# Where the weight tiles stand relative to the activation tiles, modulo 256 bytes

## The chip, the cores and the metric

One core of a Trainium2 chip runs the whole program. The metric is the device time of one execution in microseconds. Three executions of the kernel before took 1433.52, 1434.24 and 1435.65 us, median 1434.24 us.

## What is computed

Two transformer blocks of two layers each follow each other on 256 positions of width 1,024, in float32. Cut to the matrix products, one layer of the first block is:

```python
proj = rms_norm(x) @ w_in                      # 1024 x 5120
y = gate_a * (dilated_attention(...) @ w_proj_a) + gate_b * (stick_breaking_attention(...) @ w_proj_b)
x = x + y @ w_out                              # 1024 x 1024
up = rms_norm(x) @ w_up                        # 1024 x 5632
x = x + (silu(conv(up[:, :2816])) * up[:, 2816:]) @ w_down   # 2816 x 1024
...
x = x + norm(mixer(norm(x)))                   # second block, two kinds of mixer
x = x + norm(memory_cross_attention(norm(x), mem))
x = x + norm(square(relu(norm(x) @ mlp_w1)) @ mlp_w2)        # 1024 x 4096, 4096 x 1024
```

Every weight is used once, so the weights (some 230 MB) are read from HBM once per execution.

## The kernel before, in words

**Layout.** Activations lie transposed, with the 1,024 features on partitions in eight chunks of 128 and the 256 positions along the free dimension. All big products run on TensorE in the type float32r, in three terms: each operand is held as a rounded part (hi) and the rest (lo), and `mm3` (L240 to L243) issues hi x hi, lo x hi and hi x lo into the same bank, each through `mm` (L235, whose matmul is L236).

**Weights.** `plan()` lists the weights in 434 blocks in the order of use, each 512 KB or less. `prep` (L188 to L201) loads one block by DMA into a `raw` tile (three buffers), cuts it in two halves along the contraction, and for each half makes a tile `w`: ScalarE writes the hi part (L199), VectorE the lo part (L200). There are eight slots for `w` (`WB`, L35), taken in turn. A `w` tile holds up to 4,096 bytes a partition; in one pair of blocks (260 columns) it holds 4,160, and so all eight slots have that size. `take` (L203) hands a block's tiles to the product and `ahead` (L211) keeps `prep` five blocks (`LEAD`) in front.

**The products.** In `proj_t` (L288) the weights are the stationary operand (128 columns, loaded anew by each matmul) and the activations the moving one (256 columns). One `w` tile serves 12 matmuls in a row, one turn of the eight slots 96. So run the 22 pairs of `w_up` in two layers (1,056 matmuls a layer), the 16 of `w1` in two layers (768 a layer), the gates of `w_in`, and most products of the mixers. `proj_wide` (L324), used by `proj_tail` for `w_out`, `w_down` and `w2`, alternates a matmul of 512 columns (hi and lo of the activations at once) with one of 256, a pair for each 128 rows of the contraction. In `proj_n` (L334) the activations are stationary and the weights move (512 columns).

**Addresses.** Activations as operands of these products are `xh` tiles of two pools of slots: `xs` (four slots, the normalised input, L615 and `operand`) and `hs` (16 slots, everything else: `ya`, `yb`, `ox`, `lat`, the hidden layers). A slot's address within a partition is fixed when the program is built. In the built program before, the first `w` slot stands at byte 39,552 and the others each 4,160 bytes on, so modulo 256 the eight stand at 128, 192, 0, 64, 128, 192, 0, 64. All `xs` slots stand at 128 and all `hs` slots at 64. The tiles' inner offsets (hi, lo, chunk, column block) are all multiples of 256. So what this text calls the **distance** of a `w` tile from the activations it meets (its address minus theirs, modulo 256) is 0, 64, 128 or 192, the same for all the matmuls of that tile, and each occurs in two of eight slots. The profile shows no addresses; which distance a stretch has is read from the order of the built program.

Small tiles of softmax and norms are in 16 slots `sm` (L642 to L675 and others), each as large as the largest of them, `ra` and `rb` of the rotary embedding (`rope_unit`, L671; 512 bytes).

Of the kernel before, what the change touches and what calls it, by code (L numbers as in the profile page):

```python
# [10 lines left out]
F32 = mybir.dt.float32  # L11
F32R = mybir.dt.float32r
# [7 lines left out]
P = 128  # L20
# [12 lines left out]
TWO_PI = (6.28125, 0.0019350051879882812, 3.0199159819567e-07)  # L33
LEAD = 5
WB = 8  # L35
TCARGS = dict(schedule_with_timeline_sim=True)
SET_EXP = "natural_log_exp_and_others"

# [77 lines left out]
def starts(blocks):  # L116

    out = [0]
    for _, _, nk, _, C in blocks:
# [1 line left out]
    return out  # L121


BUFS = {"x": 5, "xs": 4, "hs": 16, "ft": 7, "sq": 2, "p": 6, "bias": 3, "row": 4, "sm": 16, "mk": 2, "mv": 2,
        "mm": 2, "sc": 2, "pT": 2, "pv": 1, "ms": 1}


# [1 line left out]
def net(ctx, tc, A, out):  # L129
# [3 lines left out]
    wp = ctx.enter_context(tc.tile_pool(name="wts", bufs=1))  # L133
    ap = ctx.enter_context(tc.tile_pool(name="acts", bufs=1))
    pp = ctx.enter_context(tc.tile_pool(name="psum", bufs=1, space=PSUM))
    dp = ctx.enter_context(tc.tile_pool(name="dram", bufs=1, space=DRAM))

    def f(x):
        return x.bitcast(F32)

    def sb(tag, name, shape=(2, T), dt=F32):
        return ap.tile([P] + list(shape), dt, tag=tag, name=name, bufs=BUFS[tag])

    halves = {}

    def single(group, name):

        if group in halves:
            return halves.pop(group)
        t = ap.tile([P, 2, 2, T], F32, tag="hs", name=name, bufs=BUFS["hs"])  # L150
        halves[group] = t[:, 1]
        return t[:, 0]

    def split_pair(tag, name):

        return ap.tile([P, 2, 2, T], F32R, tag=tag, name=name, bufs=BUFS[tag])

    def bank(tag, name, shape=(2, T), part=P):
        return pp.tile([part] + list(shape), F32, tag=tag, name=name, bufs=BUFS[tag])

# [27 lines left out]
    def prep(i, pieces=1):  # L188
        name, k0, nk, c0, C = W[i]
        raw = wp.tile([P, nk, C], F32, tag="raw", name=f"raw{i}", bufs=3)  # L190
        src = A["wt"][start[i]:start[i] + P * nk * C].rearrange("(p k c) -> p k c", p=P, k=nk)
        for a in range(0, nk, max(1, nk // pieces)):
            nc.sync.dma_start(raw[:, a:a + max(1, nk // pieces)], src[:, a:a + max(1, nk // pieces)])
        h = max(1, nk // 2)
        ready[i] = []
        for a, b in ((0, h), (h, nk)):
            if a < b:
                w = wp.tile([P, 2, b - a, C], F32R, tag="w", name=f"w{i}", bufs=WB)
                act.activation(w[:, 0], raw[:, a:b], AF.Copy)  # L199
                dve.tensor_tensor(w[:, 1], raw[:, a:b], f(w[:, 0]), op=OP.subtract)  # L200
                ready[i] += [w[:, :, k] for k in range(b - a)]  # L201

    def take(name, c0, k0=0):  # L203

        i = state["n"]
        assert (W[i][0], W[i][3], W[i][1]) == (name, c0, k0), (W[i], name, c0, k0)
        state["n"] += 1
        ahead()
        return ready.pop(i)

    def ahead():  # L211
        while state["next"] < max(state["n"], min(state["limit"], state["n"] + LEAD)):
            prep(state["next"])
            state["next"] += 1
# [70 lines left out]
    def col(c):  # L285
        return slice(c * P, c * P + P)
# [93 lines left out]
    x = [sb("x", f"x{j}") for j in range(4)]  # L380
# [3 lines left out]
    nc.scalar.dma_start(vec, A["vecs"])  # L384
    nc.sync.dma_start(x[0], xt[:, 0:2])
    prep(0, 2)
    state["next"] = 1
    for j in range(1, 4):
# [7 lines left out]
    def const(name, shape, q=nc.sync):  # L396
        t = cp.tile(list(shape), F32, name=name)
        q.dma_start(t, A[name])
        return t

    invf = const("invf", [P, 8], nc.gpsimd)
    prep(1)
    prep(2)
    state["next"] = 3

    def vcol(c, n=1):
        return vec[:, c:c + n]
# [74 lines left out]
    def tr(o, i):  # L482
        pe.transpose(o, i, ident)  # L483
# [128 lines left out]
        return t[hh * 64:hh * 64 + 64, c]  # L612


    h = Split("xs")  # L615
    for c in range(8):
        split_last = h.chunk(c, x[c // 2][:, c % 2], vcol(V_MIX + c))

    def first_sums():
# [4 lines left out]
        ns.chunk(x[3][:, 1])  # L624
        return ns

    exchange = const("exchange", [P, P], nc.gpsimd)
    table = const("table", [32, 28], nc.gpsimd)
    sink = cp.tile([P, 16], F32, name="sink")
# [38 lines left out]
    for l in range(DEPTH):  # L668
        vb = l * V_L1
        w_in = f"w_in{l}"  # L670
        def rope_unit(nat):  # L671
            ra = sb("sm", "ra", (2, 4, 2, 8))
            rb = sb("sm", "rb", (2, 4, 2, 8))
            for i in range(2):
                rt = nat[:, i].rearrange("p (h d) -> p h d", h=4)[:, :, 0:16]  # L675
                rt = rt.rearrange("p h (b r) -> p h b r", b=2)
                dve.tensor_tensor(ra[:, i], rt, trig[:, 0, i][:, None].to_broadcast([P, 4, 2, 8]), op=OP.mult)
                for b in range(2):
                    dve.tensor_tensor(rb[:, i, :, b], rt[:, :, 1 - b],
                                      trig[:, 1, i, b][:, None].to_broadcast([P, 4, 8]), op=OP.mult)  # L680
                dve.tensor_tensor(rt, ra[:, i], rb[:, i], op=OP.add)
            pt = bank("pT", "qT")
            for c in range(2):
                for i in range(2):
                    tr(pt[:, c, col(i)], nat[:, i, col(c)])
            s = single("rope", "qTs")
            act.activation(s, pt, AF.Copy)
            return s
# [37 lines left out]
        for u in range(3):  # L726
            if u:
                o = unit(u)
            qk += [rope_unit(n) for n in nat_units(u, o, [sb("ft", "nat"), sb("ft", "nat")])]
# [135 lines left out]
        def residual(w, y, k, gains):  # L865

            hn = Split("xs") if gains is not None else None
            ns = Sums()
            xn = []

            def on_part(c, a, b):
                if c % 2 == 0:
                    xn.append(sb("x", f"x{c // 2}"))
                t = xn[c // 2][:, c % 2]
                state["block1"] = dve.tensor_tensor(t, x[c // 2][:, c % 2], a, op=OP.add).ins
                if b is not None:
                    dve.tensor_tensor(t, t, b, op=OP.add)
                if c < 6 and c % 2:
                    ns.pair(xn[c // 2])
                if hn is not None:  # L880
                    hn.chunk(c, t, gains(c))
                if c >= 6:
                    ns.chunk(t)

            proj_tail(w, y, k, on_part)
            hold(False)
            return xn, hn, ns

        x, h, nrm = residual(f"w_out{l}", mixed, KC, lambda c: vcol(vb + V_FFN + c))
        table_set(SET_EXP)  # L890
        hh = Split("hs")
        for j in range(11):
# [6 lines left out]
            a = sb("ft", "fa")  # L899
            dve.tensor_tensor(a, o, over(rr), op=OP.mult)  # L900
            t = sb("ft", "ftt")
            for c in range(2):
                ch = 2 * j + c
                w = [vcol(vb + V_CW + 22 * q + ch) for q in range(3)]
# [22 lines left out]
        x, h, nrm = residual(f"w_down{l}", hh, FC, None if last else (lambda c: vcol(V_L1 + V_MIX + c)))  # L927
# [30 lines left out]
    hm = mem_operand(0, mem)  # L958


    lprod = sb("sm", "lp", (64,))
    lsum = sb("sm", "ls", (2,))
    for j in range(2):
        no_sync(dve.tensor_tensor_reduce(lprod, lamv[:, 2 * j], lamv[:, 2 * j + 1], 1.0, 0.0, op0=OP.mult,
# [69 lines left out]
    mk = sb("mk", "mk")  # L1034
# [3 lines left out]
    x = xn  # L1038
# [330 lines left out]
    for l in range(DEPTH):  # L1369
        name, oo, of = even(h, nrm) if l == 0 else odd(h, nrm)  # L1370
# [8 lines left out]
        x = xn  # L1379
# [9 lines left out]
        w = [take(f"xa_wo{l}", 0), take(f"xa_wo{l}", 512)]  # L1389
# [12 lines left out]
        x = xn  # L1402
# [14 lines left out]
        if l + 1 < DEPTH:  # L1417
            hm = mem_operand(1, mem)
            r = y.sums.rows(1)
            mk = sb("mk", "mk")  # L1420
            mem_keys(1, hm, mk, 0)
            h, nrm = operand(close(y, r), lambda c: gain2(l + 1, 0, c))
            x = xn
# [110 lines left out]
```

## Time and profile before

| | |
|---|---|
| median of three executions | 1434.24 us (1433.52 to 1435.65) |
| the profiled execution's own time | 1434.43 us |
| its span, first to last instruction | 1432.3 us |
| mean granted TensorE clock | 0.99 of 2.4 GHz |
| HBM read | 233.35 MB, 164 GB/s over the span |

The span is what the profile shows; 2.1 us of the execution's own time lie around it. PE in the rows is TensorE's matmuls and PEld its weight loads, DVE is VectorE and ACT ScalarE. The ends of matmuls in the profile are modelled (a record lasts some 0.28 us, while the next begins after 0.11 us), so the pace of matmuls is read from their starts: in a window that opens at the start of one matmul and closes at the start of another, the matmuls begun are the row's count less two (in a few rows less three), those whose records were still open when it opened.

### The profile page before, as it was taken

Reading aid. Unit: us, or ns where it says so; the run is one execution under the profiler, and the core shown is the slowest. Engines: PE = TensorE matmul, PEld = TensorE weight load, DVE = VectorE, ACT = ScalarE, POOL = GpSimd, SP = SyncE. Lnnn points to the kernel's source line nnn. Section 1 sums busy time; section 2 is a strip of 40 time slices with the busy share of each in tenths; the row PEclk is TensorE's granted clock in tenths of the full one; section 3 lists DMA queues with packets and bytes.
Section 4 is the critical chain, followed back from the end, with each engine's and each line's share of the span. In section 5 each row is a group of like instructions: output and inputs, shape, how many; then the busy total and the mean of one; then the engine's idle time right before and its main releaser. Section 6 shows DMA issues by size and latency. Waiting matters only on the chain.

```text
span 1432.3 us, 26226 instructions
## 1 busy us (share of the span) xinstructions
PE 1388.8 (97%) x9950; PEld 1270.7 (89%) x9950; DVE 1019.8 (71%) x2140; ACT 886.3 (62%) x1740; POOL 27.3 (2%) x54
## 2 busy tenths in 40 slices
PE   8999999999999999999999989899999999899997
PEld 6789999998888999999899968799989878799886
DVE  6665888886656578888777786777656876777554
ACT  6666566665566666666656656566556676576553
POOL 1000000000000000000000010000000010000000
PEclk9999999999999999999999989999999999999999
DMA  7543566556653455656655553266656534265662
GB/s 247 187 124 119 182 195 191 188 177 188 192 170 119 127 172 188 193 190 198 198 167 164 154 139 118 75 190 186 186 187 180 161 94 133 82 186 189 182 189 85
DMA packets 69326, 236.14 MB, mean 165 GB/s; under 512 B 7954, under 2 KB 12322, under 8 KB 69200
## 3 DMA queue, kind: packets, MB, share of 16 engines
q1 hardware_dynamic: 67136, 229.24, 51.6%
q0 software_dynamic: 1920, 5.04, 1.8%
q8 instruction: 78, 1.28, 0.4%
q14 instruction: 48, 0.39, 0.1%
q10 hardware_dynamic: 144, 0.19, 0.0%
HBM read 233.35 MB, written 1.09 MB: 164 GB/s over the span
## 4 chain that ended last, share of the span: by engine, by line
issue 53%; PE 39%; DVE 3%; ACT 3%; DMA 1%; POOL 0%; SPq 0%; DVEq 0%; POOLq 0%; ACTq 0%
PE mm L236 21%; PE mw L236 12%; PE mo L236 2%; PE ssum L427 1%; PE pT L483 1%; PE sc L607 1%; PE sc L604 1%; ACT w L199 1%; DVE w L200 1%; PE pv L541 1%; DMA bias<-brel_d 1%; DMA x<-in_xT_dram 0%; ACT rstd L176 0%; ACT sq L431 0%; ACT px L176 0%
## 5 line engine op out<-in xcount | busy, mean ns | idle before, releaser
L200 DVE TENSOR_TENSOR w<-raw,w 128x512 fp32r<-128x512 f32 (+2 forms) x866 | 585.3, 686 | 303.3 <-ACT w L199 292.8
L199 ACT ACTIVATE w<-raw 128x512 fp32r<-128x512 f32 (+2 forms) x866 | 535.5, 626 | 414.6 <-PE mm L236 225.5
L236 PE MATMUL mm<-xh,w 128*128 128x256 f32 x5892 | 722.8, 283 | 7.8 <-ACT xh L1000 6.8
L236 PEld LDWEIGHTS mm<-xh,w 128*128 128x128 f32 x5892 | 703.7, 190 | 21.2 <-ACT xh L1000 8.4
L236 PE MATMUL mw<-xh,w 128*128 128x512 f32 (+1 forms) x1832 | 327.3, 339 | 2.4 <-DVE xh L271 1.4
L236 PEld LDWEIGHTS mw<-xh,w 128*128 128x128 f32 x1832 | 281.2, 188 | 44.6 <-DVE xh L271 2.0
L236 PE MATMUL mm<-w,xh 128*128 128x512 f32 (+2 forms) x672 | 145.8, 372 | 9.5 <-ACT w L199 7.0
L236 PEld LDWEIGHTS mm<-w,xh 128*128 128x128 f32 x672 | 113.6, 191 | 34.0 <-ACT w L199 8.4
L236 PE MATMUL mo<-xh,w 128*128 128x256 f32 x192 | 30.6, 307 | 0.5 <-ACT xh L513 0.5
L236 PEld LDWEIGHTS mo<-xh,w 128*128 128x128 f32 x192 | 26.5, 206 | 4.4 <-ACT xh L513 1.7
L1000 ACT ACTIVATE xh<-x,vec 128x256 fp32r<-128x256 f32 x48 | 22.6, 501 | 10.4 <-DVE x L1365 9.9
L497 POOL DMA_DIRECT2D bias<-brel_d x28 | 14.9, 538 | 680.0 <-DVE sbb L821 293.0
L905 ACT ACTIVATE ftt<-fa,vec 128x256 f32<-128x256 f32 x44 | 24.1, 594 | 2.3 <-DVE fa L900 0.5
L1003 DVE SCALAR_TENSOR_TENSOR xh<-x,vec,xh 128x256 fp32r<-128x256 f32 x48 | 22.1, 483 | 1.1 <-ACT xh L1000 1.1
L431 ACT ACTIVATE sq<-x 128x512 f32<-128x512 f32 x33 | 20.4, 617 | 2.3 <-DMA x<-in_xT_dram 2.1
L906 DVE SCALAR_TENSOR_TENSOR ftt<-fa,vec,ftt 128x255 f32<-128x255 f32 x44 | 20.9, 482 | 0.2
L907 DVE SCALAR_TENSOR_TENSOR ftt<-fa,vec,ftt 128x254 f32<-128x254 f32 x44 | 21.0, 477 | 0.0
L703 DVE TENSOR_TENSOR gate<-mm,rstd 128x512 f32<-128x512 f32 x16 | 11.1, 691 | 12.5 <-PE mm L236 12.5
L438 DVE TENSOR_TENSOR sq<-sq 128x512 f32<-128x512 f32 x26 | 17.9, 688 | 0.0
L176 ACT ACTIVATE ftt<-ftt 128x512 f32<-128x512 f32 x22 | 13.9, 631 | 6.4 <-DVE ftt L907 6.4
L1364 DVE TENSOR_TENSOR y<-y,rstd 128x512 f32<-128x512 f32 (+1 forms) x25 | 14.5, 581 | 4.3 <-ACT rstd L176 4.1
L910 DVE TENSOR_TENSOR fa<-mm,rstd 128x512 f32<-128x512 f32 x22 | 15.1, 687 | 3.1 <-PE mm L236 3.1
(413 smaller groups left out, 1137.2 us busy)
## 6 DMA issues: line engine op xcount, KB each, us to landing
raw<-in_wt_dram SPq DMA_DIRECT2D x411, 512.0 KB, 3.6
raw<-in_wt_dram SPq DMA_DIRECT2D x16, 384.0 KB, 3.5
bias<-brel_d POOLq DMA_DIRECT2D x28, 128.0 KB, 3.4
raw<-in_wt_dram SPq DMA_DIRECT2D x4, 520.0 KB, 3.5
mem<-in_memT_dram SPq DMA_DIRECT2D x8, 256.0 KB, 4.2
x<-in_xT_dram SPq DMA_DIRECT2D x4, 256.0 KB, 6.7
raw<-in_wt_dram SPq DMA_DIRECT2D x4, 256.0 KB, 3.3
out_dram<-y SPq DMA_DIRECT2D x4, 256.0 KB, 2.5
```

Source lines behind the costliest of these rows:

```text
L199: act.activation(w[:, 0], raw[:, a:b], AF.Copy)
L200: dve.tensor_tensor(w[:, 1], raw[:, a:b], f(w[:, 0]), op=OP.subtract)
L236: i = pe.matmul(o, a, b, start=start, stop=stop, skip_group_check=True).ins
L431: act.activation(sq, src, AF.Square)
L438: dve.tensor_tensor(self.acc, self.acc, sq, op=OP.add)
L497: nc.gpsimd.dma_start(o, src)
L905: act.activation(t[:, c], a[:, c], AF.Identity, bias=vcol(vb + V_CB + ch), scale=w[2])
L906: dve.scalar_tensor_tensor(t[:, c, 1:], a[:, c, :T - 1], w[1], t[:, c, 1:], op0=OP.mult, op1=OP.add)
L907: dve.scalar_tensor_tensor(t[:, c, 2:], a[:, c, :T - 2], w[0], t[:, c, 2:], op0=OP.mult, op1=OP.add)
L910: dve.tensor_tensor(a, o, over(rr), op=OP.mult)
L1000: act.activation(hi, t, AF.Copy, scale=g)
L1003: return dve.scalar_tensor_tensor(lo, t, g, f(hi), op0=OP.mult, op1=OP.subtract)
```

## The change

The `w` slots become 4,224 bytes (`W_SLOT` = 1,056 elements), of which a tile uses as much as before. Two spare tiles (`pad`) of 192 and 64 bytes are put ahead of and behind the `xs` slots. The small tiles `ra`, `rb` and `lp` move from the 16 slots `sm` to four slots of their own, `ro`, so that an `sm` slot shrinks from 512 to 64 bytes.

```diff
+W_SLOT = 1056
...
-BUFS = {..., "sm": 16, "mk": 2, ...
+BUFS = {..., "sm": 16, "ro": 4, "mk": 2, ...
...
+    def pad(name, n):
+        ap.tile([P, n // 4], F32, tag=name, name=name, bufs=1)
...
-                w = wp.tile([P, 2, b - a, C], F32R, tag="w", name=f"w{i}", bufs=WB)
+                w = wp.tile([P, W_SLOT], F32R, tag="w", name=f"w{i}", bufs=WB)
+                w = w[:, :2 * (b - a) * C].rearrange("p (s k c) -> p s k c", s=2, k=b - a)
...
+    pad("pad0", 192)
     h = Split("xs")
...
+    pad("pad1", 64)
...
-            ra = sb("sm", "ra", (2, 4, 2, 8))
-            rb = sb("sm", "rb", (2, 4, 2, 8))
+            ra = sb("ro", "ra", (2, 4, 2, 8))
+            rb = sb("ro", "rb", (2, 4, 2, 8))
...
-    lprod = sb("sm", "lp", (64,))
+    lprod = sb("ro", "lp", (64,))
```

In the built program after, the `w` slots stand at 128 and 0 in turn modulo 256, and all `xs` and `hs` slots at 64. The distance is therefore 64 or 192, each in four of eight slots, and never 0 or 128. The slots `raw`, `x`, `sq`, `row`, `p`, `bias`, `ft` and the constants stand where they stood modulo 256. On every engine and in the queue of SP the same instructions follow in the same order, row for row; some of VectorE's rotary instructions have one more wait, for VectorE's own earlier ones (`ra` and `rb` come round after two uses, where a slot of `sm` came round after more).

## Rows read from the trace of the kernel before

**Rows 1.** The page's first part: busy us (share of the span), instructions.

```profile
PE 1388.8 (97%) x9950; PEld 1270.7 (89%) x9950; DVE 1019.8 (71%) x2140; ACT 886.3 (62%) x1740; POOL 27.3 (2%) x54
```

**Rows 2.** Waits of the whole span: engine, line, waited for: us, times, longest us.

```profile
ACT w L199 <- PE mm L236: 225.5, 315, 3.6
...
ACT w L199 <- DMA raw<-in_wt_dram: 30.5, 23, 4.6
...
PE mm L236 <- ACT w L199: 7.5, 4, 6.1
```

**Rows 3.** Groups of L236 by form: count, busy us, mean ns, idle before.

```profile
L236 PE MATMUL mm<-xh,w 128*128 128x256 f32 x5892 | 722.8, 283 | 7.8 <-ACT xh L1000 6.8 <-ACT w L199 0.5 <-DVE xh L1003 0.4
...
L236 PE MATMUL mw<-xh,w 128*128 128x256 f32 x916 | 257.3, 282 | 0.0
L236 PE MATMUL mm<-w,xh 128*128 128x512 f32 x480 | 120.4, 405 | 7.0 <-ACT w L199 7.0
```

**Rows 4.** Windows, w_up0 and three mixers: length, busy by engine, clock, DMA share, GB/s.

```profile
187.40:313.10 125.70, 125.70 (x1063) 124.62 (x1063) 105.71 (x182) 81.60 (x139) 1.62 (x3) 1.00 0.60 188
6.10:152.40 146.30, 145.34 (x944) 124.87 (x945) 93.57 (x234) 94.79 (x190) 4.29 (x8) 1.00 0.54 173
738.10:922.90 184.80, 169.41 (x1219) 150.20 (x1218) 137.70 (x395) 114.24 (x277) 8.86 (x17) 0.96 0.46 134
1105.70:1237.80 132.10, 122.30 (x880) 104.02 (x878) 97.38 (x277) 86.67 (x224) 6.01 (x12) 1.00 0.42 123
```

**Rows 5.** Windows of L236 alone in w_up0: distances 192, 64, 0, 128; one turn.

```profile
203.34:204.76 1.42, 1.42 (x14) 1.42 (x13) 1.00 0.17 52
204.76:207.48 2.72, 2.72 (x26) 2.72 (x25) 1.00 0.90 265
207.48:208.91 1.43, 1.43 (x14) 1.43 (x13) 1.00 0.81 321
208.91:210.33 1.42, 1.42 (x14) 1.42 (x13) 1.00 0.70 147
230.00:241.26 11.26, 11.26 (x98) 11.26 (x97) 1.00 0.63 187
```

**Rows 6.** The same in w1 of layer 0: distances 64, 192, 64, 192; one turn.

```profile
1005.55:1006.97 1.42, 1.42 (x14) 1.42 (x13) 1.00 0.45 136
1006.97:1008.38 1.41, 1.41 (x14) 1.41 (x13) 1.00 0.59 227
1008.38:1009.75 1.37, 1.37 (x14) 1.37 (x13) 1.00 0.66 150
1009.75:1011.11 1.36, 1.36 (x14) 1.36 (x13) 1.00 0.60 232
940.78:952.05 11.27, 11.27 (x98) 11.27 (x97) 1.00 0.72 214
```

**Rows 7.** The same: a turn of w_up1; a turn of w1 layer 1, its distances 64, 192.

```profile
596.70:607.86 11.16, 11.16 (x98) 11.16 (x97) 1.00 0.61 190
1288.38:1299.75 11.37, 11.37 (x99) 11.37 (x98) 1.00 0.63 187
1289.81:1292.63 2.82, 2.82 (x26) 2.82 (x25) 1.00 0.66 202
1296.91:1299.75 2.84, 2.84 (x27) 2.84 (x26) 1.00 0.63 185
```

**Rows 8.** The same in proj_wide: a turn of w2; its distances 64, 192; 64 in w_down1.

```profile
1033.79:1045.07 11.28, 11.28 (x67) 9.83 (x65) 1.00 0.57 169
1045.07:1047.89 2.82, 2.82 (x18) 2.45 (x17) 1.00 0.70 228
1047.89:1050.72 2.83, 2.83 (x18) 2.46 (x17) 1.00 0.69 224
686.88:688.27 1.39, 1.39 (x10) 1.23 (x9) 1.00 0.73 254
```

**Rows 9.** The same: proj_n in w_in0, distances 0 and 64 in turn.

```profile
44.58:50.15 5.57, 5.57 (x26) 4.51 (x24) 1.00 0.62 194
```

More of the change, by code (lines that the diff above doesn't have):

```diff
@@ L121, in starts @@
     return out
-BUFS = {"x": 5, "xs": 4, "hs": 16, "ft": 7, "sq": 2, "p": 6, "bias": 3, "row": 4, "sm": 16, "mk": 2, "mv": 2,
+BUFS = {"x": 5, "xs": 4, "hs": 16, "ft": 7, "sq": 2, "p": 6, "bias": 3, "row": 4, "sm": 16, "ro": 4, "mk": 2, "mv": 2,
         "mm": 2, "sc": 2, "pT": 2, "pv": 1, "ms": 1}
```

## The prediction

> **What bounds the kernel now.** I read the page's first part, then the waits, the groups of L236, and windows of a few microseconds.
>
> The first part puts PE at 97% of the span and DVE, next, at 71% [rows 1]. Busy PE alone proves little, as the ends of its records are modelled. The waits settle it: ScalarE's writing of `w` waits 225.5 us for the products of `mm` (it wants a slot that the matmuls still read), 30.5 us for the weights' DMA, and the matmuls wait only 7.5 us for `w` [rows 2]. Weights are ready ahead of use and slots come free too late. In w_up0 PE is busy all of 125.70 us, DVE 105.71, the DMA engines 0.60 of the time [rows 4]. So the pace of matmuls sets the time, and what the change can touch is that pace: it moves addresses, and no instruction.
>
> Now the pace, from windows that open and close at a matmul's start. One `w` tile is 12 matmuls of 256 columns. In w_up0 [rows 5] a tile at distance 192 takes 1.42 us (118.3 ns a matmul), the two tiles at 64 behind it 2.72 us for 24 (113.3 ns), then one at 0 takes 1.43 us (119.2) and one at 128 1.42 us (118.3). The granted clock is 1.00 (2.4 GHz) in all of them, so it is not the clock. A turn of eight slots, 96 matmuls, takes 11.26 us, 117.3 ns each.
>
> One distance does not always have one pace. In w1 of layer 0 [rows 6] four tiles follow each other at 64, 192, 64, 192: 1.42, 1.41, 1.37, 1.36 us. In w1 of layer 1 [rows 7] tiles at 64 and at 192 take 2.82 and 2.84 us for 24, 117.9 ns both. So 64 and 192 each have a **fast** pace (113.3 ns) and a **slow** one (117.9), and keep over a tile, and into the next, the one they came in with; 0 and 128 have no fast pace: no such tile in these stages goes below 1.41 us, and the first tile behind one comes in fast or slow. What a border between 64 and 192 does is what the changed kernel will be made of. Two stages show it. A slow 192 before a 64 turned fast 17 times of 17 (first at 203.34, last at 1006.97 [rows 5, 6]); a fast 64 stayed fast into 192 7 times of 7 in w1 of layer 0 (last at 1008.38 [rows 6]); a slow 64 stayed slow into 192 6 times of 6 (last at 1005.55 [rows 6]). In the trace as a whole I found no fast 192 that turned slow at a 64, though only three such borders, and two slow 192s that stayed slow.
>
> **The change, part by part.**
>
> *Distances 0 and 128 go.* Tiles stand at 64 and 192 alone. By the borders above, slow is left at the first step from 192 to 64, and fast is not left. A turn in the fast pace is 96 x 113.3 = 10.88 us. Against it stand turns of 11.26 (w_up0), 11.16 (w_up1), 11.27 and 11.37 us (w1) [rows 5 to 7]. With 1,056 / 96 = 11 turns in each w_up and 768 / 96 = 8 in each w1 that gives 11 x 0.38 + 11 x 0.28 + 8 x 0.39 + 8 x 0.49 = 14.3 us. Each stage may begin slow for half a turn, 4 x 0.5 x (11.32 - 10.88) = 0.9 us. I take **13.4**.
>
> *The other 256-column products.* All groups of this kind hold 6,384 matmuls (5,892 of them in the largest [rows 3]). Less the 3,648 above, 1,152 are in w_in and w_pa, w_pb, where PE is busy 145.34 of 146.30 us [rows 4]. Other matmuls interrupt these runs often and can bring them in slow, so I count three quarters at 113.3 and one at 117.9, mean 114.4, against 117.3: 1,152 x 2.9 = **3.3**. Another 1,212 are in the second block's mixers and its attention to memory, where PE idles 15.4 of 184.8 and 9.8 of 132.1 us [rows 4] and waits on chains through ScalarE and VectorE; a faster product there partly lengthens such a wait. Half: 1,212 x 2.9 / 2 = **1.7**. The last 128 columns of each `proj_tail`, 372 matmuls, enter from alternating ones; half fast, 372 x 1.7 = **0.6**.
>
> *proj_wide.* It alternates 512 and 256 columns, 916 pairs [rows 3]. A turn of 32 pairs takes 11.28 us, 352.5 ns a pair; of its distances, 64 takes 2.82 us for 8 (352.5) and 192 2.83 (353.8) [rows 8]. So I take (352.5 + 353.8) / 2 = 353.1 and **+0.6** us. The bounds: 64 has been seen at 1.39 us for 4, 347.5 [rows 8], which for all pairs is 916 x 5 = 4.6 us less, and all at 353.8 is 1.2 more.
>
> *proj_n.* Weights move and activations stand: 480 matmuls of 512 columns, at 5.57 us for 24, 232 ns [rows 9]; distances 0 and 64 alternate there within the run, and I saw no pace that goes with either. **0**. If it found a fast pace too, of 2 x 113.3 = 226.6, 480 x 5.4 = 2.6 us less; no row shows it slower than now.
>
> *The small tiles.* `ra` and `rb` in four slots make some of VectorE's instructions wait for VectorE itself, which works in order; nothing else is queued differently. The spare bytes cost no instruction. **0**.
>
> *Cover.* Nothing is costed at zero because it is hidden, but the gain needs weights that keep up. At 10.88 us a turn, w_up0 would last 11 x 10.88 = 119.7 us, DVE would be busy 105.7 of that, 88%, and the DMA engines 0.63.
>
> Sum: 13.4 + 3.3 + 1.7 + 0.6 - 0.6 = 18.4 us less. From the profiled execution's 1434.43, which is 0.2 above the median, that is **1416.0 us**.
>
> **A rule against the change.** The windows show the weight load of the next matmul under the current one, and a pace that goes with the addresses of the two: 113.3 to 119.2 ns [rows 5]. The Trainium skill, "TensorE: Matmul & The Clock Gate", section "Step-by-step: what each phase is for", says that TensorE reads SBUF through two independent ports and "Loading the next tile's weights doesn't steal SBUF read bandwidth from the running matmul"; its section "Back-to-back issue gap" gives 262 cycles for 256 columns, 109.2 ns, wherever they stand. By that the change would do nothing (the last rival). The trace disagrees as far as pace goes with distance: no window here is at 109.2.
>
> **The rivals.**
>
> *Locked slow* (slower). If the slow pace survives the border from 192 to 64, nothing in the changed kernel ever sets the fast one: before, a 64 tile came in fast from 128 too, and a 192 tile from 0 (w_up1, whose turn is the shortest [rows 7]), and those ways are gone. For it: w1 of layer 1 is slow at 64 and 192 throughout [rows 7], and two borders stayed slow. Against it: 17 of 17 in the FFN stages. It would put 6,384 matmuls at 117.9 against 117.3, 3.8 us, and with 1.1 for proj_wide gives 1434.4 + 4.9 = 1439. It decides if under about one turn in ten of a stage finds fast.
>
> *Half the gain* (faster). Either fast is lost more often than three borders can show, or, with PE 3% faster, slots and weights come just in time and VectorE at 88% makes matmuls wait in places. For it: PE in w_up leaves DVE little room. Against: ScalarE's 225.5 us of waiting for slots [rows 2]. With half of 18.4 it gives 1425.
>
> *No change.* The pace might go with a tile's place in the turn, with what ScalarE, VectorE and the DMAs write at that moment, and not with its distance; then the turns stay at their 11.16 to 11.37 us and the time at 1434.4. Against: a tile at 0 or 128 is never fast whatever the stage, and the DMA rate beside the fast windows is anything from 150 to 265 GB/s [rows 5, 6].
>
> **How the numbers follow.** A measurement of this kernel can tell about 0.2% (2.9 us) from no change. Forecast 0.76, half the gain 0.12, locked slow 0.08, no change 0.04. Locked slow is the only case over 1437, so slower 0.08; no change and a sliver of half the gain make same 0.05; faster 0.87. Bounds of the forecast: fast everywhere from the start and all of it on the path is 14.3 + (1,152 + 1,212 + 372) x 4.0 / 1000 = 25.2 us, with 4.6 and 2.6 from proj_wide and proj_n 32, hence 1402, all at once unlikely; with the mixers at nothing and proj_wide at its worst 13.4 - 1.2 = 12.2, hence 1422. The range is 1406 to 1427: it leaves out the extreme low end and the last two rivals, and takes in half the gain.
>
> **What would show it.** A turn of w_up and of w1 should take 10.9 us in all four stages, w_up 120 us instead of 125.70, and tiles at 64 and 192 alike 1.36. Turns of w2 should stay at 11.3. ScalarE's waits for slots should fall only a little. Turns at 11.3 in the FFN stages mean locked slow; long stretches of both paces mean half the gain; turns in w_up that differ as before, that distance was not the cause.

## The result, and the profile after

Four executions of the changed kernel took 1415.67, 1416.15, 1419.11 and 1421.28 us, median 1417.63; four of the kernel before, beside them, had the median 1433.88. The ratio is 0.9888, 95% interval 0.9863 to 0.9912: about 1.1% faster, and 1.6 us above the forecast of 1416.0. The profiled execution took 1419.11 us, its span is 1417.3 us. The new lines move the code: L236 is now L242, ScalarE's and VectorE's writing of `w` (L199, L200) are L205 and L206.

The page's first part of the changed kernel (busy us, share, instructions) answers [rows 1]; all counts are the same, and PE loses 16.6 us of busy time:

```profile
PE 1372.2 (97%) x9950; PEld 1253.5 (88%) x9950; DVE 1017.7 (72%) x2140; ACT 887.3 (63%) x1740; POOL 27.4 (2%) x54
```

Its waits, for [rows 2] (us, times, longest us):

```profile
ACT w L205 <- PE mm L242: 203.1, 288, 3.6
...
ACT w L205 <- DMA raw<-in_wt_dram: 28.8, 22, 6.1
...
PE mm L242 <- ACT w L205: 7.9, 4, 6.1
```

ScalarE still waits 203.1 us for slots (225.5 before), and the matmuls wait 7.9 us for `w` (7.5 before), so weights are still ready ahead of use and the matmuls still set the time.

Windows of the matmuls of L242 alone in the changed kernel, opened and closed at starts as in [rows 5 to 8]. In order: in w_up0 two tiles at distance 192, the tile at 64 right behind, and a later one at 192; then a turn of eight slots in w_up0, w_up1, w1 of layer 0, w1 of layer 1; last 32 pairs of w2. A row gives the window, its length, the busy time of PE and of PEld with their counts, the granted clock, the DMA share and GB/s.

```profile
203.88:205.30 1.42, 1.42 (x14) 1.42 (x13) 1.00 0.36 35
206.71:208.12 1.41, 1.41 (x14) 1.41 (x13) 1.00 0.95 206
208.12:209.48 1.36, 1.36 (x14) 1.36 (x13) 1.00 0.90 361
210.84:212.20 1.36, 1.36 (x14) 1.36 (x13) 1.00 0.76 280
208.12:219.00 10.88, 10.88 (x98) 10.88 (x97) 1.00 0.72 218
584.74:595.62 10.88, 10.88 (x98) 10.88 (x97) 1.00 0.63 192
950.12:961.00 10.88, 10.88 (x98) 10.88 (x97) 1.00 0.62 195
1258.77:1269.65 10.88, 10.88 (x98) 10.88 (x97) 1.00 0.63 194
1010.17:1021.47 11.30, 11.30 (x66) 9.83 (x65) 1.00 0.60 184
```

These rows show the forecast mechanism. The stage comes in slow (1.42 us a tile), at 208.12 a slow 192 is followed by a 64, and from there every tile takes 1.360 us whatever its distance. (Slots do not come up in the order of their addresses: the distances named here and in the run with all eight distances fit the order 192, 192, 192, 64, 64, 192, 64, 64 in w_up0, with two borders from 192 to 64 in a turn.) A turn is 10.88 us in all four FFN stages, where it was 11.16 to 11.37 [rows 5 to 7]. The pairs of w2 stay at 11.30.

Whole stages for [rows 4], busy time of PE, PEld, DVE, ACT and POOL in turn: w_up0, w_up1, w_in0 and the second block's two mixers.

```profile
188.10:310.00 121.90, 121.90 (x1063) 120.82 (x1062) 104.86 (x182) 81.89 (x139) 1.63 (x3) 1.00 0.62 194
547.80:669.00 121.20, 121.06 (x1062) 120.78 (x1061) 104.33 (x182) 82.54 (x141) 0.00 (x0) 1.00 0.61 193
6.10:153.30 147.20, 145.90 (x944) 125.37 (x945) 93.39 (x234) 95.01 (x190) 4.29 (x8) 1.00 0.54 172
730.80:914.60 183.80, 168.10 (x1220) 148.91 (x1218) 137.38 (x395) 114.40 (x277) 8.87 (x17) 0.96 0.46 135
1094.70:1226.20 131.50, 121.58 (x880) 103.25 (x878) 97.68 (x277) 86.49 (x224) 6.01 (x12) 1.00 0.40 124
```

w_up0 went from 125.70 to 121.90 us with PE still busy throughout, the mixers from 184.8 to 183.8 and from 132.1 to 131.5. But w_in0 did not get shorter (146.30 before, 147.20 now), although its matmuls of 256 columns went from 116.7 to 114.5 ns. The loss lies in the first 18 us. Between 16 and 18 us of the span, the matmuls that began (with the few still open) and PE alone, first before:

```profile
16.00:18.00 2.00, 2.00 (x14) 1.00 0.84 270
```

The changed kernel:

```profile
16.00:18.00 2.00, 2.00 (x7) 1.00 0.88 276
```

The changed kernel run again in the last experiment:

```profile
16.00:18.00 2.00, 2.00 (x15) 1.00 0.90 301
```

At the start of each profiled execution the matmuls of 512 columns begin 427 ns apart, later 231 ns. In this execution of the changed kernel the first short distance begins at 17.7 us, before at 13.2, and the matmul that began at 16.04 us before began at 18.14: 2.1 us lost, in this execution and not in the repeat, where it began at 14.98. The granted clock stands at 1.00 in these rows, so they do not say what delays the step; the second weight tile was later here (the matmuls went on at 9.18 us instead of 8.72). It is no effect of the change: the repeat, with the same program, has the first short distance at 12.1 us and took 1415.49 us, and in the traces of the nine other kernels it begins at 10.4 to 13.2 us.

### The profile page after: what moved, and what is told of

Same layout as the page of the kernel before. It is cut to its first block, busy times and chain, and to the rows that moved or that the text cites. A ratio compares the mean times of both kernels' runs of the same rounds, so it can differ in the third digit from the quotient of the medians.

```text
span 1417.3 us, 26235 instructions
## 1 busy us (share of the span) xinstructions
PE 1372.2 (97%) x9950; PEld 1253.5 (88%) x9950; DVE 1017.7 (72%) x2140; ACT 887.3 (63%) x1740; POOL 27.4 (2%) x54
## 4 chain that ended last, share of the span: by engine, by line
issue 53%; PE 38%; DVE 4%; ACT 3%; DMA 1%; POOL 0%; SPq 0%; DVEq 0%; POOLq 0%; ACTq 0%
PE mm L242 20%; PE mw L242 12%; PE mo L242 2%; PE ssum L433 1%; ACT w L205 1%; DVE w L206 1%; DMA raw<-in_wt_dram 1%; PE pT L489 1%; PE pv L547 1%; PE sc L613 1%; PE sc L610 1%; DMA bias<-brel_d 1%; ACT sq L437 1%; ACT rstd L181 0%; ACT px L181 0%
## 5 line engine op out<-in xcount | busy, mean ns | idle before, releaser
L206 DVE TENSOR_TENSOR w<-raw,w 128x512 fp32r<-128x512 f32 (+2 forms) x866 | 584.2, 684 | 292.9 <-ACT w L205 287.9
L205 ACT ACTIVATE w<-raw 128x512 fp32r<-128x512 f32 (+2 forms) x866 | 535.7, 626 | 397.1 <-PE mm L242 203.1
L242 PE MATMUL mm<-xh,w 128*128 128x256 f32 x5892 | 705.0, 280 | 8.0 <-ACT xh L1008 6.9
L242 PEld LDWEIGHTS mm<-xh,w 128*128 128x128 f32 x5892 | 686.2, 189 | 21.4 <-ACT xh L1008 8.5
L242 PE MATMUL mw<-xh,w 128*128 128x512 f32 (+1 forms) x1832 | 328.3, 339 | 3.0 <-DVE xh L277 2.0
L242 PEld LDWEIGHTS mw<-xh,w 128*128 128x128 f32 x1832 | 281.4, 188 | 45.9 <-DVE xh L277 2.7
L242 PE MATMUL mm<-w,xh 128*128 128x512 f32 (+2 forms) x672 | 147.0, 374 | 10.0 <-ACT w L205 7.4
L242 PEld LDWEIGHTS mm<-w,xh 128*128 128x128 f32 x672 | 114.9, 193 | 34.3 <-ACT w L205 8.8
L242 PE MATMUL mo<-xh,w 128*128 128x256 f32 x192 | 30.5, 306 | 0.5 <-ACT xh L519 0.5
L242 PEld LDWEIGHTS mo<-xh,w 128*128 128x128 f32 x192 | 26.4, 205 | 4.4 <-ACT xh L519 1.7
L444 DVE TENSOR_TENSOR sq<-sq 128x512 f32<-128x512 f32 x26 | 17.8, 684 | 0.0
```

What stands on the lines that cost most here:

```text
L242: i = pe.matmul(o, a, b, start=start, stop=stop, skip_group_check=True).ins
L444: dve.tensor_tensor(self.acc, self.acc, sq, op=OP.add)
```

## The experiments

Each is an edit of the changed kernel. Times are medians with their range; ratios are to runs of the kernel before on the same chip, with the 95% interval. "Mean pace" is the mean distance between starts of 256-column matmuls of a `w` tile over the whole trace: 117.39 ns before, 114.34 in the changed kernel; a "pair" in `proj_wide` took 351.6 ns before and 352.8 in the changed kernel.

**The other two distances.** 64 spare bytes ahead of the slots and 192 behind: the tiles stand at distances 128 and 0 alone.

```diff
+                if i == 0 and a == 0:
+                    wp.tile([P, 16], F32, tag="lead", name="lead", bufs=1)
...
+    pad("pad2", 192)
```

> The changed kernel with the eight weight slots moved on by 64 bytes and nothing else moved: distances 128 and 0 alone, slots still 4,224 bytes apart. Theory (distance): no fast pace anywhere, a tile of 12 takes 1.42 to 1.44 us everywhere, 118.9 ns a matmul against 114.3 in the changed kernel; 6,384 x 4.6 ns = 29 us more than 1417.6, about 1445 (1440 to 1450), slower than the kernel before. Rival (it is the even spacing of 4,224 bytes, the smaller slots, or anything else of the change but the distance): 1418, as the changed kernel.

Measured: 1443.98 us (1442.52 to 1445.12), ratio 1.0072 (1.0050 to 1.0094). In its w_up0 a tile at 0, one at 128, and a turn (matmuls alone):

```profile
226.70:228.14 1.44, 1.44 (x14) 1.44 (x13) 1.00 0.88 299
231.02:232.43 1.41, 1.41 (x14) 1.41 (x13) 1.00 0.39 58
226.70:238.14 11.44, 11.44 (x98) 11.44 (x97) 1.00 0.59 187
```

Mean pace 119.13 ns: 6,384 x (119.13 - 117.39) = 11.1 us more, and the time rose by 10. The same slots, spare bytes and small tiles, moved by 64 bytes, turn a gain of 16 us into a loss of 10. So the distances decide, and not the 4,224 bytes from slot to slot.

**192 alone.** Slots of 4,352 bytes, a multiple of 256, with 128 bytes ahead and behind. This takes the border from 192 to 64 away, which is the case of the rival *locked slow*.

```diff
-W_SLOT = 1056
+W_SLOT = 1088
...
+                if i == 0 and a == 0:
+                    wp.tile([P, 32], F32, tag="lead", name="lead", bufs=1)
...
+    pad("pad2", 128)
```

> Slots 4,352 bytes apart and all at distance 192; the rest of the changed kernel stands where it stood modulo 256. Theory (the pace is kept, and the slow one is left only at a border from 192 to 64): runs that begin at 192 begin slow (12 of 12 in the kernel before), there is no such border, so everything stays at 117.9 ns: 6,384 x 3.6 ns = 23 us over 1417.6, about 1440 (1434 to 1443). Rival (192 and 64 are simply good distances, and the slow stretches have another cause): about 1418, with fast and slow stretches as before.

Measured: 1435.20 us (1433.60 to 1437.11), ratio 1.0009 (0.9997 to 1.0022). A turn in w_up0, one in w1 of layer 0, and 32 pairs of w2:

```profile
225.96:237.27 11.31, 11.31 (x98) 11.31 (x97) 1.00 0.60 188
945.69:957.00 11.31, 11.31 (x99) 11.31 (x98) 1.00 0.68 213
...
1017.77:1028.93 11.16, 11.16 (x66) 9.77 (x65) 1.00 0.61 185
```

The FFN stages ran at 117.8 ns from end to end, 96% of all starts in the slow pace; of 338 borders entered slow none was left fast. The gain is gone with the border. About half of what it stayed under 1440 is the pairs: 350.0 ns against 352.8, 916 x 2.8 = 2.6 us, which I had not priced; most of the rest is the pace, 117.61 ns on average and not 117.9, 6,384 x 0.29 = 1.9 us.

**64 alone.** The same slots without the bytes ahead.

```diff
-W_SLOT = 1056
+W_SLOT = 1088
```

> Slots 4,352 bytes apart and all at distance 64. Theory (the pace is kept): each run of matmuls keeps the pace that it begins with; runs at 64 begin fast in 11 of 17 cases of the kernel before, so long stretches of either pace, each FFN stage wholly fast or wholly slow from its last interruption on: 1412 to 1441, likeliest about 1425, and no step from slow to fast inside a stretch without an interruption. Rival (64 and 192 are simply good distances): about 1418.

Measured: 1427.67 us (1422.51 to 1428.58), ratio 0.9952 (0.9935 to 0.9968). A turn in w_up0 and one in w1 of layer 0:

```profile
225.92:237.22 11.30, 11.30 (x98) 11.30 (x97) 1.00 0.58 187
946.70:957.58 10.88, 10.88 (x98) 10.88 (x97) 1.00 0.64 215
```

The same distance, the same instructions, two paces: both w_up stages ran slow to their end, both w1 stages fast. Of 340 borders from 64 to 64, 127 stayed fast, 213 stayed slow and none changed. So the pace is kept, and is not a mean of something varying; the alternation in the changed kernel is what repairs a slow start.

**4,160-byte slots again.** Spare bytes and small slots stay as in the changed kernel, only the slots go back.

```diff
-W_SLOT = 1056
+W_SLOT = 1040
```

> The changed kernel with the weight slots 4,160 bytes apart again, all four distances in turn as before; spare bytes and smaller slots kept. Theory (distance): a turn of w_up takes 11.2 to 11.4 us again, and the time is that of the kernel before, 1434 (1430 to 1438). Rival (spare bytes or smaller slots bring it): 1418.

Measured: 1437.73 us (1436.61 to 1441.97), ratio 1.0028 (1.0015 to 1.0041). Turns in w_up0 and w1 of layer 0:

```profile
225.17:236.53 11.36, 11.36 (x98) 11.36 (x97) 1.00 0.54 188
946.60:957.98 11.38, 11.38 (x98) 11.38 (x97) 1.00 0.69 210
```

The other parts of the change bring nothing alone; they place the activations. It is even 4 us slower than before: all four distances are there again, and mean pace is 118.01 ns, 6,384 x 0.62 = 4.0 us. Before, all `xs` slots stood 64 bytes further on than `hs`; now they stand together, so the products from `xs` meet the four distances in another order of slots.

**Everything 64 bytes further.** The slots move by 64 and all that lies behind them too, so distances stay and addresses change.

```diff
+                if i == 0 and a == 0:
+                    wp.tile([P, 16], F32, tag="lead", name="lead", bufs=1)
```

> The changed kernel with 64 spare bytes ahead of the weight slots: weights at 192 and 64 modulo 256, activations at 128, everything behind moved on by 64; the distances stay 64 and 192. Theory (distance): as the changed kernel, 1418 (1414 to 1422). Rival (what counts is where weights or activations stand by themselves: weights at 0 and 128, or activations at 64): the fast pace goes, 1435 to 1445.

Measured: 1417.91 us (1416.44 to 1418.35), ratio 0.9882 (0.9867 to 0.9897), mean pace 114.47 ns, the changed kernel's within what separates two executions. Turns in w_up0 and w1 of layer 0:

```profile
225.53:236.41 10.88, 10.88 (x98) 10.88 (x97) 1.00 0.57 188
955.32:966.20 10.88, 10.88 (x98) 10.88 (x97) 1.00 0.67 196
```

It is the difference of the two addresses that counts. The kernel with distances 128 and 0 has the same 64 bytes ahead, and its weights stand where they stand here; it differs by the 192 bytes behind the slots alone, which move the activations (and what lies behind them), and took 1443.98 us.

**All eight multiples of 32.** Slots of 4,192 bytes.

```diff
-W_SLOT = 1056
+W_SLOT = 1048
```

> The changed kernel with slots 4,192 bytes apart: the eight slots have the eight distances that are multiples of 32. It measures the paces of 32, 96, 160 and 224, which no run has shown. Theory: tiles at 0 and 128 stay at 1.42 to 1.44 us, those at 64 and 192 at 1.36 or 1.41. If the pace changes smoothly with distance, 32 and 96 lie between their neighbours and the time near 1433 (1428 to 1440); if grains of 64 bytes decide, 32 and 160 run as 0 and 128 do, 96 and 224 as 64 and 192, and the time is also near 1433; the tiles tell these apart.

Measured: 1436.84 us (1435.18 to 1439.85), ratio 1.0020 (1.0009 to 1.0030). A turn in w_up0 in order of time, distances 160, 192, 0, 96, 64, 128, 224, 32:

```profile
228.67:230.11 1.44, 1.44 (x14) 1.44 (x13) 1.00 0.83 290
230.11:231.52 1.41, 1.41 (x14) 1.41 (x13) 1.00 0.39 73
231.52:232.95 1.43, 1.43 (x14) 1.43 (x13) 1.00 0.84 309
232.95:234.36 1.41, 1.41 (x14) 1.41 (x13) 1.00 0.20 49
234.36:235.74 1.38, 1.38 (x14) 1.38 (x13) 1.00 0.92 243
235.74:237.15 1.41, 1.41 (x14) 1.41 (x13) 1.00 0.50 139
237.15:238.57 1.42, 1.42 (x14) 1.42 (x13) 1.00 0.79 277
238.57:239.99 1.42, 1.42 (x14) 1.42 (x13) 1.00 0.46 95
```

Over the trace the median tile stands at 119.5 ns for distance 0, 118.3 for 32, 117.8 for 64, 117.4 for 96, 118.6 for 128, 119.6 for 160, 117.7 for 192 and 117.0 for 224; only 64 and 192 have tiles at 113.4 to 113.9, while the quickest at 224 is 116.3. So the time was as expected, but neither simple picture of the cause fits: not a smooth curve (224 has the lowest median and no fast pace), and not grains of 64 bytes (0 and 32 would share one, and 128 and 160, yet 32 is 1.2 ns quicker than 0 and 160 is 1.0 ns slower than 128).

**hi and lo apart.** If the border from 192 to 64 repairs the pace, it can stand inside every triple of `mm3`: 128 spare bytes between a tile's hi and lo part put hi at 64 and lo at 192 in every slot.

```diff
-W_SLOT = 1056
+W_SLOT = 1088
...
-                w = w[:, :2 * (b - a) * C].rearrange("p (s k c) -> p s k c", s=2, k=b - a)
+                n = (b - a) * C
+                g = 32 if C != 260 else 0
+                w = w[:, :2 * (n + g)].rearrange("p (s n) -> p s n", s=2)[:, :, :n]
+                w = w.rearrange("p s (k c) -> p s k c", k=b - a)
```

> Slots 4,352 bytes apart, and within each weight tile 128 spare bytes between the hi and the lo part: hi at distance 64, lo at 192, so that of three matmuls two are at 64 and one at 192, and each triple holds a border from 192 to 64. Theory (such a border turns slow into fast): slow stretches end within a few matmuls everywhere; 6,384 matmuls at 113.4 to 114 ns instead of 114.3, 2 to 6 us less than 1417.6, about 1413 (1410 to 1416). Rival (a border acts only where matmuls at one distance have gone before for a while): paces mixed as in the changed kernel or slow, 1418 to 1435.

Measured: 1415.05 us (1413.90 to 1416.55), ratio 0.9865 (0.9846 to 0.9884), mean pace 113.94, 10% of starts slow. A turn in w_up0, and 32 pairs of w2:

```profile
225.11:235.99 10.88, 10.88 (x98) 10.88 (x97) 1.00 0.59 196
...
1015.23:1026.54 11.31, 11.31 (x66) 9.92 (x65) 1.00 0.57 181
```

Slow starts are repaired sooner, within a tile or two, and the one fast stretch that turned slow in w_up0 (at 203 us) was fast again nine matmuls on; 6,384 x (114.34 - 113.94) = 2.6 us. The times alone do not tell this kernel from the changed one (1415.67 to 1421.28 and, run again below, 1413.98 to 1418.19); the paces do.

**The same the other way round.** 128 bytes more ahead of the slots (and behind) put hi at 192 and lo at 64; the rest of the edit is the same.

```diff
+                if i == 0 and a == 0:
+                    wp.tile([P, 32], F32, tag="lead", name="lead", bufs=1)
...
+    pad("pad2", 128)
```

> The same with hi at distance 192 and lo at 64: two matmuls of three at 192. Theory: each triple holds a border from 192 to 64 here too, so about 1413 (1410 to 1417). Rival (the part at which two of three matmuls stand sets the pace, as the runs at 64 or 192 alone did): slow, about 1430, while the kernel with hi at 64 is nearer 1420.

Measured: 1420.84 us (1418.11 to 1426.77), ratio 0.9910 (0.9879 to 0.9940); the profiled execution is the slowest, 1426.77. A turn in w_up0, one in w1 of layer 0, and 32 pairs of w2:

```profile
226.38:237.80 11.42, 11.42 (x98) 11.42 (x97) 1.00 0.58 183
955.40:966.28 10.88, 10.88 (x98) 10.88 (x97) 1.00 0.62 201
1015.27:1026.36 11.09, 11.09 (x66) 9.77 (x65) 1.00 0.64 199
```

A miss, and one that limits the theory. Each triple holds a border from 192 to 64 here too, yet w_up0 is slow throughout, with starts 118, 118 and then 118 or 125 ns apart, and w1 fast throughout. With two of three matmuls at 192 the border repairs next to nothing: behind the first few matmuls of a run, slow turned fast at two places alone, six matmuls before the sums for the norm in each w_up (195.9 and 560.8 us). Elsewhere the pace is kept again. So "a 64 behind a slow 192 turns fast" does not hold for a single matmul at 64. The surprise is in the pairs: 347.7 ns over the trace, where the kernels above had about 350 to 353.

**Each where it is quick.** hi at 64 and lo at 192 as in the former edit but one, and in the blocks of `w_out`, `w_down` and `w2`, which `proj_wide` uses, hi at 192 and lo at 64.

```diff
-W_SLOT = 1056
+W_SLOT = 1152
...
+                o = 32 if name[:-1] in ("w_out", "w_down", "w2") else 0
+                w = w[:, o:o + 2 * (n + g)].rearrange("p (s n) -> p s n", s=2)[:, :, :n]
```

> The kernel with hi at 64 and lo at 192, but in the blocks of w_out, w_down and w2 hi at 192 and lo at 64, as those of the other order had their pairs of 512 and 256 columns at 347.7 ns against 352.9. Theory (the pace of a pair goes with its two distances): 916 pairs x 5.2 ns = 4.8 us less than 1415.05, 1410 (1407 to 1413), faster than the changed kernel by some 7 us. Rival (the pairs were quicker for another cause in that run): 1415.

Measured: **1410.13 us** (1408.88 to 1412.33), ratio 0.9832 (0.9816 to 0.9849). 32 pairs of w2:

```profile
1016.05:1027.14 11.09, 11.09 (x66) 9.76 (x65) 1.00 0.58 171
```

Pairs at 347.1 ns against 352.9 with hi at 64: 916 x 5.8 = 5.3 us, and 4.9 us is what the median fell against the former edit but one (that ran on another chip, where the kernel before took 1434.85 us; beside this one it took 1434.12). This version beats both kernels, the changed one by some 6 us.

**The changed kernel again**, beside it.

> The changed kernel once more beside it: 1417.6 (1415 to 1421), with the FFN stages wholly at 113.3 ns but for their first turn.

Measured: 1416.26 us (1413.98 to 1418.19), ratio 0.9874 (0.9853 to 0.9895). Its FFN stages come in as in the first trace: w_up0 and w1 of layer 0 slow for half a turn or so, and all four at 113.3 ns from there to their end.

## Why the prediction was right

*What bounds it.* Right. A 3% quicker stream of matmuls shortened the stages it fills by as much, and ScalarE still waits 203.1 us for slots.

*The terms.* From the starts of matmuls in the two traces:

| term | predicted us | measured us |
|---|---|---|
| turns of the four FFN stages | -13.4 | -13.2 |
| w_in, w_pa, w_pb | -3.3 | -3.3 |
| second block's mixers and attention | -1.7 | -1.6 |
| last chunk of proj_tail | -0.6 | -0.9 |
| proj_wide | +0.6 | +1.1 |
| sum | -18.4 | -17.9 |

The FFN term is the change of mean pace times the matmuls: w_up0 117.26 to 113.65, w_up1 116.36 to 113.55 (1,056 each), w1 117.32 to 113.78 and 118.39 to 113.57 (768 each). For w_in the guess that a quarter of the matmuls would be slow, at 114.4 ns on average, met 114.49 and 114.92. The mixers' term is the difference of the two windows, and there the number came right by luck: I had a pace 2.9 ns quicker of which half is lost in waits, but the matmuls that follow each other without a wait went only from 117.6 to 116.0 ns, 1,212 x 1.6 = 1.9 us, and most of that arrived. proj_n, put at nothing, went from 231.4 to 230.7 ns a matmul, some 0.3 us. The last chunks gained half as much again as I had. proj_wide was the term most mis-sized: pairs at 192 took 353.7 ns in the changed kernel, close to the row I had, but the kernel before had 351.6 over all of them where the one turn I read had 352.5, so the rise was 1.2 ns a pair where I had 0.6.

The profiled executions differ by 1434.43 - 1419.11 = 15.3 us, 2.6 short of that sum; 2.1 of it is the late step at the start. The repeat is 18.9 us under 1434.43, and 1.1 of that is its early step (14.98 against 16.04 us), which leaves 17.8.

*The borders.* The forecast rested on 17 borders of one kind and only 3 of the weakest. The changed kernel has 178 that can be counted. Counting tiles of uninterrupted runs by the pace before and behind a border: fast stayed fast at 72 of 72 borders from 192 to 64 and 85 of 85 from 64 to 192; a slow 64 stayed slow into 192 at 8 of 8; a slow 192 turned fast at a 64 at 10 of 13. That is the rule of the prediction, with the leak it had seen (slow 192s that stayed slow), here 3 of 13.

*One number of "what would show it" was wrong.* I gave 120 us for w_up0, 11 turns alone. The stage also holds about 2 us of other products (the sums for the norm), inside 125.70 as well; 125.70 less 11 x 0.38 is 121.5, and 121.90 is what came.

*The rivals.* *Locked slow* is a real mechanism: with 192 alone it happened throughout, at 1435.2 instead of my 1439. It did not happen here because the border is there in each turn. *Half the gain* did not come: no stage fell back. *No change* is excluded by three kernels with the same instructions: 1443.98 with distances 0 and 128, 1435.20 with 192, 1417.91 with both moved. The Trainium skill's rule on loading weights ("TensorE: Matmul & The Clock Gate", section "Step-by-step: what each phase is for"), that the load takes no read bandwidth from the running matmul, was read in the prediction as a reason for no change. The runs do not bear that reading out: the pace runs from 113.3 to 119.6 ns, and where these kernels differ is the two operands' addresses. Whether it is read bandwidth that the two operands share, no run shows. The 262 cycles that the prediction took from the Trainium skill (same page, section "Back-to-back issue gap") are its figure for the isolated gap of single matmuls; the best pace in these runs, with a weight load for each matmul, is 113.3 ns.

## What to carry to other kernels

When a stage is nothing but matmuls and still varies by a few per cent between tiles of one shape, list the starts by the addresses of both operands modulo 256 before looking at other engines. Here, for weights of 128 columns loaded anew for each matmul of 256, the stationary tile should stand 64 or 192 bytes behind the moving one (modulo 256), with both occurring, because a pace once found is kept within a run, and in the changed kernel it was a border from 192 to 64 that repaired a slow one; hi at 64 and lo at 192 does that within each tile (1415.05, not clearly quicker than the changed kernel), and the opposite where 512 and 256 columns alternate (1410.13 us together). Test such a layout by moving one side by 64 bytes and by moving both: if the distance is the cause, the first changes the time and the second does not.

## What the runs showed that I had not expected

- The pace of one loop of equal matmuls has two values that persist for a hundred microseconds: 113.3 and 117.8 ns at distance 64, in different stages of one execution, with nothing between. What picks it when a run begins stays open; executions of the kernel with hi at 192 differ by 8.7 us, more than those of any other.
- Pairs of 512 and 256 columns have paces of their own, 347.1 to 353.7 ns, and favour the layout with hi at 192 and lo at 64 that the 256-column runs don't. In the run with all eight distances 224 (347.3) and 96 (348.0) were the quickest. One distance has more than one pace here too: at 192 a pair took 353.7 ns in the changed kernel and 350.0 where all tiles stand at 192. Why is open.
- Why the distance matters was not found. The runs show that it is a difference of the two operands' addresses and that 64 and 192 stand out; whether the two reads share anything was not tried.
- The step from 427 to 231 ns a matmul at the start came at 10.4 to 13.2 us in eleven profiled executions and at 17.7 in one, worth 2 us, more than any but the two largest terms of this change.
